# Kept weight sums of two wide gate products, requested earlier on the synchronous queue

## The chip, the cores and the metric

The kernel runs on one core of a Trainium2 chip. The metric is the device time of one execution in microseconds, as the median of several. Its engines work side by side and meet at semaphores: TensorE (PE) multiplies, ScalarE (ACT) and VectorE (DVE) prepare operands and empty the PSUM banks, GpSimd (POOL) and SyncE (SP) mostly issue DMAs.

## What is computed

One layer of an encoder on 256 positions with a model width of 2048, all in float32: a combined projection, two branches, a merge by sigmoid gates, an output projection, then a convolutional gated MLP and a final norm. The part that matters here is the gates:

```
h = rms_norm(x, g_norm)                      # 256 x 2048
proj = h @ w_in                              # 2048 x 9216
uv, qkv, gates = jnp.split(proj, [2 * GM_WIDTH, 2 * GM_WIDTH + 3 * NA_WIDTH], axis=-1)
...
g_a, g_b = jnp.split(jax.nn.sigmoid(gates), 2, axis=-1)
merged = g_a * (y_a @ w_branch[:GM_WIDTH]) + g_b * (y_b @ w_branch[GM_WIDTH:])
return x + merged @ w_out
```

Each gate has 2048 columns. The stages below compute the right halves, 1024 columns of each gate: 256 x 2048 by 2048 x 1024, twice.

## The kernel before

**Three products for one.** Every float32 operand is split into a high part (rounded by ScalarE, `whi`) and a low remainder (subtracted by VectorE, `wlo`), and a product is three matmuls: high by high, low by high, high by low (lines 317 to 319).

**A wide stage.** The right half of a gate is one call of `wide` and one of `run_wide`. Its weights come as 16 pieces, one for each 128 rows: 128 x 1024 floats, 512 KB, into one of five buffers `wraw`. Here the pieces are called a0 to a15 for the first gate and b0 to b15 for the second, in the order in which they are worked off; two neighbours with even start are a pair. Six of the eight pairs of a gate are multiplied with seven block products in place of eight, by a Strassen-Winograd scheme: it needs four sums of the pair's weight blocks (`weight_sums`, lines 360 to 364 on VectorE, split by `weight_sums_split`, lines 374 and 375) and four sums of the pair's activation blocks, the x sums. An even piece of such a pair has 9 matmuls, an odd one 12; a plain piece has 12. All eight PSUM banks are held by a stage: four for products P, four for results C. At the end of a stage `post_sums` (lines 595 to 599) and `add_sums` (line 604) empty them on ScalarE and VectorE, and the next stage starts in the banks that come free.

**What is kept.** For two pairs of each gate (pair 0 and pair 3, counted by rows of the weights) the weight sums were made and split much earlier, and written to DRAM as four tiles of 512 KB: `gate_h13`, `gate_l13`, `gate_h24`, `gate_l24`. The stage reads them back into `kh13`, `kl13`, `kh24` and `kl24`, which have one buffer each, used by all four of these pairs in turn. Of such a pair the first piece is loaded by half (256 KB). The x sums of all pairs were kept in DRAM too and are read back into three tiles s0, s1 and s2, in the turn that `GATE_TILES` gives; a tile that still holds the wanted pair is used again.

In the first gate, a2 and a3 are pair 0 and a10 and a11 are pair 3, both kept; a8 and a9 are pair 6, a12 and a13 pair 4. In the second, b2 and b3 are pair 3 and b10 and b11 are pair 0, both kept; b8 and b9 are pair 1, b12 and b13 pair 2.

**The order.** The program is written out in the order of pieces. `begin(i)` requests loads up to four pieces ahead, splits weights up to three pieces ahead, and then runs the tasks that are due at piece i. A read that is to be made n pieces ahead is a task at i - n. All these requests, weights, kept sums and x sums, go to one queue, SP's (lines 145, 1258, 1271), which issues them one after the other: a request waits until its tile is free (and until the DMA eight before it, whose semaphore it takes over, has landed), and those behind it wait too.

The leads stand in `GATE_SPLIT`: for each gate, a map from pair to three numbers, the lead of the x sums, of the tiles 13 and of the tiles 24. `wide` takes them up so:

```
ready = split[0].get(k // 2) if split else None
at(i - (ready[0] if ready else lead), ... stored(k // 2, b["acts"]))
...
    for n, lead in zip(("13", "24"), ready[-2:]):
        at(i - lead, lambda b=b, k=k, n=n: split[1](k // 2, b, n))
```

The loop uses the name `lead` again, so after a kept pair the x sums of the following pairs of the same stage are requested with that pair's last number as their lead.

Of the kernel before, what the change touches and what calls it, by code (L numbers as in the profile page):

```python
# [50 lines left out]
GATE_KEPT, GATE_MADE = (1, 2, 6), (0, 3, 4)  # L51
GATE_QUADS = ((0, 1, 2, 4, 5, 6),) * 2
GATE_ORDER = ((2, 3, 0, 1, 4, 5, 10, 11, 12, 13, 6, 7, 8, 9, 14, 15), (8, 9, 6, 7, 12, 13, 14, 15, 2, 3, 0, 1, 4, 5, 10, 11))
GATE_SPLIT = ({0: (2, 4, 3), 3: (2, 3, 2)}, {3: (2, 2, 2), 0: (4, 2, 1)})
GATE_TILES = (0, 1, 2, 0, 1, 2, 2, 1, 0)
GATE_FIRST = (40, (44, 46, 48, 48), (49, 51))
GATE_JOB = (3, (6, 6, 7, 7), (9, 12))
# [21 lines left out]
def trunk_kernel(ctx, tc, x, x_t, vecs, w_in, ln_g, ln_b, w_st, b_s, rpb, w_branch, w_out, w_up, w_down,  # L79
# [836 lines left out]
    def ev_gate_sums(br):  # L916
        def done(P, i):
            def go():
                gate_tile(br)
                mg["x", br] = [[mg["t", br][:, t, c * 512:(c + 1) * 512] for c in range(2)] for t in range(NT)]  # L920
                post_sums(P, mg["x", br], junk)

            at(i + 1, go)
        return done

    def ev_gate_wide(br):
        def done(ps, i):
            g = mg["t", br]
            add_sums(ps, mg["x", br])

            def sigmoid():
                for t in range(NT):
                    nc.scalar.activation(g[:, t, :], g[:, t, :], AF.Sigmoid, scale=st1["r"][:, t:t + 1])

            at(i + 1, sigmoid)
            for c in range(2):
                mg[br, 2 + c] = g[:, :, c * 512:(c + 1) * 512]
        return done
# [277 lines left out]
    def sums_room(name, dt):  # L1216
        return s_room["p"].tile([128, 2, 512], dt, name=name)
# [35 lines left out]
    def split_read(kept, g, tile_of, queue=nc.gpsimd):  # L1253
        def read(pair, box, n):
            u = box.setdefault("u", [])
            u.append([tile_of(pair, p + n) for p in "hl"])
            for t, src in zip(u[-1], kept[pair, g][n]):
                queue.dma_start(t.bitcast(F32), src)
            if len(u) == 2:
                split_sums(box, u)  # L1260
        return read

    def kept_sums(pair, box):
        held = [s for p, s in gate_held.values() if p == pair]
        if held:
# [10 lines left out]
                 (ev_gate_sums(br), ev_gate_wide(br)), stored=kept_sums, lead=(2, 4)[br], behind=((), (0,))[br],  # L1276
                 split=(GATE_SPLIT[br], split_read(g_kept, br, lambda pair, name: sums_room("k" + name, F32R), nc.sync)))
            for br in range(2)]
# [41 lines left out]
    def split_rows(name, pair, g):  # L1320
        return {m: [dram.tile([128, 2, 512], F32, name=f"{name}_{h}{m}_{pair}_{g}") for h in "hl"]
                for m in ("13", "24")}
# [10 lines left out]
    for n, (pair, g) in enumerate((pair, g) for g in range(2) for pair in OUT_SPLIT[g]):  # L1333
# [3 lines left out]
                    [i + a for a in OUT_JOB[2]], 4, last=True)  # L1337
    for n, (pair, br) in enumerate((pair, br) for br in range(2) for pair in GATE_SPLIT[br]):
        g_kept[pair, br] = split_rows("gate", pair, br)
# [258 lines left out]
```

## Time and profile before

| | |
|---|---|
| median of three runs | 1290.16 us (1289.01 to 1290.35) |
| the profiled execution | 1290.33 us, 1288.5 of it the span of the core |
| granted TensorE clock | 0.998 |
| TensorE busy | 1277.2 us, 99% of the span |
| VectorE, ScalarE busy | 1118.3 and 793.0 us |
| DMA moved | 369.51 MB, mean 287 GB/s |
| first wide gate stage (a0 to a15) | 373.3 to 412.7 us |
| second (b0 to b15) | 412.7 to 453.4 us |

A row of the timeline has the start in us, the duration in us, engine, line, operation, what is written and read, and in brackets the idle time before it with what ended it. For SP's queue a row is the issue of a DMA; when it landed stands in the DMA view. The row of a window has its length and then the busy time of each engine, with counts. Matmuls overlap, so their starts tell more than their durations.

### The profile page before, as it was taken

The page shows a single profiled execution, that of the slowest core. Times are in us where ns is not written, and L with a number is a line of the kernel's source. Part 1 is how long each engine was busy: PE and PEld are TensorE (multiplying, and loading weights), DVE is VectorE, ACT ScalarE, POOL GpSimd, SP SyncE. Part 2 cuts the span into 40 slices and gives each one's busy share as a digit, 9 for nine tenths or more (in the row PEclk, how much of TensorE's full clock was granted, in tenths as well). Part 3 has the DMA queues.
Part 4 walks back from the last instruction along what each step waited for, and adds up shares of the span by engine and source line. Part 5 has one row for each costly group of instructions (what it writes and reads, how often), then busy time and mean ns, then how long its engine had stood idle before and what let it go on. Part 6 is the DMA issues. An engine that isn't in the chain of part 4 may idle for free.

```text
span 1288.5 us, 19673 instructions
## 1 busy us (share of the span) xinstructions
PE 1277.2 (99%) x6717; PEld 1088.7 (84%) x6717; DVE 1118.3 (87%) x1644; ACT 793.0 (62%) x1179; POOL 162.1 (13%) x307
## 2 busy tenths in 40 slices
PE   9999999999999999999999999999999999999997
PEld 7888888888887888888888888888888888888885
DVE  7898977777799989996889999998988989979987
ACT  7776575775755655565665666665665656556654
POOL 0003852330000001100001000100000001211210
PEclk9999999999999999999999999999999999999999
DMA  9789889989789977965688789888776859998993
GB/s 364 278 272 284 288 263 345 341 284 321 247 314 360 347 238 262 387 215 179 193 281 286 239 275 304 272 260 291 261 227 219 279 174 359 374 387 321 353 392 132
DMA packets 199893, 369.51 MB, mean 287 GB/s; under 512 B 15984, under 2 KB 124144, under 8 KB 199792
## 3 DMA queue, kind: packets, MB, share of 16 engines
q1 hardware_dynamic: 175472, 286.36, 64.7%
q0 software_dynamic: 23888, 81.23, 17.7%
q8 instruction: 52, 0.85, 0.2%
q10 hardware_dynamic: 432, 0.66, 0.1%
q14 instruction: 49, 0.40, 0.1%
HBM read 320.48 MB, written 45.61 MB: 284 GB/s over the span
## 4 chain that ended last, share of the span: by engine, by line
PE 96%; DVE 2%; DMA 1%; issue 1%; DVEq 0%; ACT 0%; SPq 0%; ACTq 0%
PE bank L222 31%; PE bank L226 16%; PE bank L319 11%; PE bank L317 11%; PE bank L318 11%; PE bank L250 5%; PE bank L251 5%; PE bank L252 5%; DMA wraw<-in_w_down_dram 1%; DVE wlo L171 1%; PE bank L871 0%; PE bank L825 0%; PE bank L498 0%; PE bank L860 0%; PE bank L698 0%
## 5 line engine op out<-in xcount | busy, mean ns | idle before, releaser
L171 DVE TENSOR_TENSOR wlo<-wraw,whi 128x1024 fp32r<-128x1024 f32 (+1 forms) x472 | 537.4, 1152 | 125.0 <-ACT whi L170 74.8
L170 ACT ACTIVATE whi<-wraw 128x1024 fp32r<-128x1024 f32 (+1 forms) x472 | 463.8, 995 | 224.1 <-PE bank L318 65.1
L222 PE MATMUL bank<-h,whi 128*128 128x512 f32 x1760 | 423.3, 391 | 0.0
L222 PEld LDWEIGHTS bank<-h,whi 128*128 128x128 f32 x1760 | 322.7, 188 | 62.1
L226 PEld LDWEIGHTS bank<-h,wlo 128*128 128x128 f32 x1760 | 225.9, 191 | 8.8
L226 PE MATMUL bank<-h,wlo 128*128 128x256 f32 x1760 | 228.6, 283 | 0.0
L1076 ACT ACTIVATE tc<-ta,ck 128x256 f32<-128x256 f32 x86 | 47.1, 595 | 109.8 <-DVE ta L1074 109.8
L319 PE MATMUL bank<-wlo,a 128*128 128x512 f32 x188 | 73.4, 390 | 0.6 <-DVE wlo L171 0.6
L318 PE MATMUL bank<-whi,a 128*128 128x512 f32 x188 | 73.2, 389 | 0.0
L317 PE MATMUL bank<-whi,a 128*128 128x512 f32 x188 | 73.1, 389 | 0.0
L317 PE MATMUL bank<-whi,h 128*128 128x512 f32 x186 | 72.8, 392 | 0.0
L319 PE MATMUL bank<-wlo,h 128*128 128x512 f32 x186 | 72.6, 390 | 0.0
L318 PE MATMUL bank<-whi,h 128*128 128x512 f32 x186 | 72.6, 390 | 0.0
L1079 DVE SCALAR_TENSOR_TENSOR tc<-ta,ck,tc 128x255 f32<-128x255 f32 x86 | 41.4, 482 | 14.4 <-ACT tc L1076 14.4
L250 PE MATMUL bank<-whi,h 128*128 128x512 f32 x128 | 50.3, 393 | 0.0
L250 PE MATMUL bank<-whi,y 128*128 128x512 f32 x128 | 50.3, 393 | 0.0
L251 PE MATMUL bank<-whi,h 128*128 128x512 f32 x128 | 49.8, 389 | 0.0
L251 PE MATMUL bank<-whi,y 128*128 128x512 f32 x128 | 49.8, 389 | 0.0
L252 PE MATMUL bank<-wlo,h 128*128 128x512 f32 x128 | 49.8, 389 | 0.0
L252 PE MATMUL bank<-wlo,y 128*128 128x512 f32 x128 | 49.8, 389 | 0.0
L374 ACT ACTIVATE h<-h 128x1024 fp32r<-128x1024 f32 x36 | 38.1, 1059 | 17.5 <-DVE h L364 12.0
L1308 POOL DMA_DIRECT2D down_h<-so x16 | 8.7, 544 | 311.2 <-ACT tc L1086 184.9
(325 smaller groups left out, 1990.1 us busy)
## 6 DMA issues: line engine op xcount, KB each, us to landing
wraw<-in_w_up_dram SPq DMA_DIRECT2D x336, 256.0 KB, 4.1
wraw<-in_w_in_dram SPq DMA_DIRECT2D x107, 512.0 KB, 6.1
wraw<-in_w_down_dram SPq DMA_DIRECT2D x78, 512.0 KB, 7.5
wraw<-in_w_in_dram SPq DMA_DIRECT2D x70, 256.0 KB, 4.4
wraw<-in_w_branch_dram SPq DMA_DIRECT2D x32, 512.0 KB, 5.3
wraw<-in_w_out_dram SPq DMA_DIRECT2D x28, 512.0 KB, 5.9
h<-sums POOLq DMA_DIRECT2D x18, 512.0 KB, 7.5
tw<-in_w_down_dram POOLq DMA_DIRECT2D x8, 1024.0 KB, 8.9
```

The source lines that it names most:

```text
L170: nc.scalar.activation(h[:, k, :m], w[:, k, :m], AF.Copy)
L171: nc.vector.tensor_sub(l[:, k, :m], w[:, k, :m], h[:, k, :m].bitcast(F32))
L222: nc.tensor.matmul(p, h[:, k - k0, b * 128:(b + 1) * 128], acts(k), start=k == 0, stop=k == nk - 1)
L226: nc.tensor.matmul(p[:, :T], l[:, k - k0, b * 128:(b + 1) * 128], acts(k)[:, 0, :], start=False, stop=False)
L250: nc.tensor.matmul(p, xh, h[:, kk, :m], start=st, stop=False)
L251: nc.tensor.matmul(p, xl, h[:, kk, :m], start=False, stop=False)
L252: nc.tensor.matmul(p, xh, l[:, kk, :m], start=False, stop=sp)
L317: nc.tensor.matmul(p, xh, h, start=st, stop=False, **kw)
L318: nc.tensor.matmul(p, xl, h, start=False, stop=False, **kw)
L319: nc.tensor.matmul(p, xh, l, start=False, stop=sp, **kw)
L1076: nc.scalar.activation(v, u, AF.Identity, scale=ck[:, 1, ch:ch + 1], bias=ck[:, 3, ch:ch + 1])
L1079: nc.vector.scalar_tensor_tensor(v[:, 1:], u[:, :T - 1], ck[:, 0, ch:ch + 1], v[:, 1:], op0=OP.mult, op1=OP.add)
```

## The change

One line of numbers changes.

```
--- before
+++ after
-GATE_SPLIT = ({0: (2, 4, 3), 3: (2, 3, 2)}, {3: (2, 2, 2), 0: (4, 2, 1)})
+GATE_SPLIT = ({0: (2, 4, 3), 3: (2, 6, 5)}, {3: (2, 4, 3), 0: (4, 6, 5)})
```

The tiles 13 and 24 of the second kept pair of each gate are requested six and five pieces ahead, where it was three and two in the first gate and two and one in the second. Those of the second gate's first kept pair go four and three ahead, where it was two and two. By way of `lead`, x sums move too: those of pair 4 at a12 from two pieces ahead to five, those of pairs 6 and 1 in the second gate from two to three (pair 6 still lies in its tile and isn't read), those of pair 2 at b12 from one to five. Pair 4's x sums are now requested before pair 3's, so that these two swap the tiles s1 and s2. Instructions of TensorE, ScalarE, VectorE and POOL keep their order and number.

SP's queue in the first gate. Here `wraw` is the load of a piece (128x512 the half of a10), `kh` and `kl` the kept sums, `s` the x sums. Before, from the load of a9 to that of a13:

```order
L145 DMA wraw_4212<-in_w_in_dram 128x1024
L1271 DMA s0_4218<-xsums6_154 128x1024
L145 DMA wraw_4238<-in_w_in_dram 128x512
L145 DMA wraw_4264<-in_w_in_dram 128x1024
L1258 DMA kh13_4270<-gate_h13_3_0_140 128x1024
L1258 DMA kl13_4271<-gate_l13_3_0_141 128x1024
L145 DMA wraw_4286<-in_w_in_dram 128x1024
L1271 DMA s1_4292<-xsums3_156 128x1024
L1258 DMA kh24_4294<-gate_h24_3_0_142 128x1024
L1258 DMA kl24_4295<-gate_l24_3_0_143 128x1024
L145 DMA wraw_4307<-in_w_in_dram 128x1024
```

The same stretch now, from behind the load of a8 to that of a13:

```order
L1258 DMA kh13_4203<-gate_h13_3_0_140 128x1024
L1258 DMA kl13_4204<-gate_l13_3_0_141 128x1024
L145 DMA wraw_4216<-in_w_in_dram 128x1024
L1271 DMA s0_4222<-xsums6_154 128x1024
L1258 DMA kh24_4230<-gate_h24_3_0_142 128x1024
L1258 DMA kl24_4231<-gate_l24_3_0_143 128x1024
L145 DMA wraw_4246<-in_w_in_dram 128x512
L145 DMA wraw_4272<-in_w_in_dram 128x1024
L1271 DMA s1_4278<-xsums4_157 128x1024
L145 DMA wraw_4292<-in_w_in_dram 128x1024
L1271 DMA s2_4298<-xsums3_156 128x1024
L145 DMA wraw_4309<-in_w_in_dram 128x1024
```

The tiles 13 have moved ahead of three loads (a9, a10, a11), the tiles 24 ahead of three (a10, a11, a12), and the x sums of pair 4, which stood behind a14, ahead of a12.

SP's queue in the second gate, before, from the load of b9 to behind that of b13:

```order
L145 DMA wraw_4580<-in_w_in_dram 128x1024
L145 DMA wraw_4604<-in_w_in_dram 128x512
L1271 DMA s2_4610<-xsums1_152 128x1024
L1271 DMA s1_4620<-xsums0_155 128x1024
L145 DMA wraw_4634<-in_w_in_dram 128x1024
L145 DMA wraw_4652<-in_w_in_dram 128x1024
L1258 DMA kh13_4658<-gate_h13_0_1_148 128x1024
L1258 DMA kl13_4659<-gate_l13_0_1_149 128x1024
L145 DMA wraw_4671<-in_w_in_dram 128x1024
L1258 DMA kh24_4677<-gate_h24_0_1_150 128x1024
L1258 DMA kl24_4678<-gate_l24_0_1_151 128x1024
```

And now, from behind the load of b8 to that of b13:

```order
L1258 DMA kh13_4571<-gate_h13_0_1_148 128x1024
L1258 DMA kl13_4572<-gate_l13_0_1_149 128x1024
L145 DMA wraw_4584<-in_w_in_dram 128x1024
L1271 DMA s2_4590<-xsums1_152 128x1024
L1258 DMA kh24_4598<-gate_h24_0_1_150 128x1024
L1258 DMA kl24_4599<-gate_l24_0_1_151 128x1024
L145 DMA wraw_4614<-in_w_in_dram 128x512
L1271 DMA s1_4628<-xsums0_155 128x1024
L145 DMA wraw_4642<-in_w_in_dram 128x1024
L1271 DMA s0_4648<-xsums2_153 128x1024
L145 DMA wraw_4662<-in_w_in_dram 128x1024
L145 DMA wraw_4677<-in_w_in_dram 128x1024
```

The tiles 13 have moved ahead of four loads (b9 to b12), the tiles 24 ahead of four (b10 to b13), and the x sums of pair 2, which stood behind b15, ahead of b12. In the first pair of this gate (not shown) the tiles 13 have moved ahead of b3 and b4, the tiles 24 ahead of b4.

## The prediction

> **What bounds the kernel now.** I read the page's shares first, then the idle time in the two wide gate stages, then the queue that feeds them.
>
> The page of the kernel before:
>
> ```profile
> span 1288.5 us, 19673 instructions
> PE 1277.2 (99%) x6717; PEld 1088.7 (84%) x6717; DVE 1118.3 (87%) x1644; ACT 793.0 (62%) x1179; POOL 162.1 (13%) x307
> ```
>
> TensorE sets the time: 1288.5 - 1277.2 = 11.3 us is all that it leaves idle. The moved reads lie in the two gate stages, a0 to a15 and b0 to b15, so the question is how much of the 11.3 us is there. Busy time by stage (us, PE, PEld, DVE, ACT, POOL, clock, DMA share, GB/s), and the waits in both stages together:
>
> ```profile
> 373.30:412.70 39.40, 39.40 (x175) 32.63 (x174) 36.20 (x46) 22.33 (x25) 0.00 (x0) 1.00 0.89 325
> 412.70:453.40 40.70, 39.80 (x176) 32.56 (x175) 38.88 (x47) 23.58 (x26) 0.56 (x1) 1.00 0.93 349
> ```
>
> ```profile
> DVE t L364 <- DMA wraw<-in_w_in_dram: 2.1, 2, 1.8
> PE bank L317 <- DVE g L604: 0.9, 1, 0.9
> ```
>
> In the first gate TensorE never idles; in the second it idles once, for 0.9 us. No row has it waiting for a kept sum. Around that one stall, TensorE and VectorE by time:
>
> ```profile
> 415.20 0.39 PE L319 MATMUL bank<-l,s 128*128 128x512 f32 x1
> 416.49 0.50 PE L317 MATMUL bank<-h,s 128*128 128x512 f32 x1 [0.90 <-DVE g L604]
> ```
>
> ```profile
> 398.34 0.69 DVE L364 TENSOR_TENSOR t<-wraw 128x512 f32<-128x512 f32 x1 [1.81 <-DMA wraw<-in_w_in_dram]
> 400.27 1.22 DVE L171 TENSOR_TENSOR wlo<-wraw,whi 128x1024 fp32r<-128x1024 f32 x1
> 413.47 2.36 DVE L375 TENSOR_TENSOR l<-t,h 128x1024 fp32r<-128x1024 f32 x2
> 415.74 2.48 DVE L604 TENSOR_TENSOR g<-bank,g 128x512 f32<-128x512 f32 x4
> ```
>
> From 415.20 to 416.49 is 1.29 us, where undisturbed matmuls start 0.23 apart (380.97 and 381.20, further down), so the stall costs 1.06 us. It waits for the first of the four L604 additions, which empty the first gate's banks. That addition is late because VectorE has worked without a break since 398.34, and it started there 1.81 us late: L364 forms a sum from a12 and a13, the last pair of the first gate, and waited for the load of a13. So **one number rules this stage: when a13 lands.** Its landing comes from the synchronous queue (start, issue time; then the times to landing, in short windows, of the issues at 376.98, at 385.08 and 385.51, and at 388.23):
>
> ```profile
> 376.98 0.33 SPq L145 DMA_DIRECT2D wraw<-in_w_in_dram  x1
> 378.83 0.33 SPq L145 DMA_DIRECT2D wraw<-in_w_in_dram  x1
> 384.66 0.33 SPq L145 DMA_DIRECT2D wraw<-in_w_in_dram  x1
> 385.08 0.38 SPq L1258 DMA_DIRECT2D kh<-gate_h  x1
> 385.51 0.42 SPq L1258 DMA_DIRECT2D kl<-gate_l  x1
> 388.23 0.39 SPq L145 DMA_DIRECT2D wraw<-in_w_in_dram  x1
> ```
>
> ```profile
> wraw<-in_w_in_dram SPq DMA_DIRECT2D x1, 512.0 KB, 3.4
> ...
> kh<-gate_h SPq DMA_DIRECT2D x1, 512.0 KB, 5.9
> kl<-gate_l SPq DMA_DIRECT2D x1, 512.0 KB, 6.6
> ...
> wraw<-in_w_in_dram SPq DMA_DIRECT2D x1, 512.0 KB, 10.1
> ```
>
> The rows at 376.98, 378.83, 384.66 and 388.23 are a8, a9, a11 and a13. So kh lands at 385.1 + 5.9 = 391.0 and a13 at 388.2 + 10.1 = 398.3, six 512 KB transfers later (kl13, a12, the x sums of pair 3, kh24, kl24, a13): 7.3 / 6 = 1.22 us each, in the order of their requests.
>
> **The change part by part.** No arithmetic changes on any engine; TensorE, ScalarE and VectorE keep their instructions and their order. What moves are requests on the synchronous queue, with as many bytes in all. Four things to price.
>
> 1. *Earlier arrival of the kept sums: 0.* The first gate's second pair is used by TensorE from about 400 on. The tile views, kh and then kl:
>
> ```profile
> L318 PE MATMUL bank<-kh,s x6: 389/389/389, 380.3 to 401.4; 128*128 128x512 f32 x6
> L1258 SPq DMA_DIRECT2D kl<-gate_l x2: 402/413/424, 385.5 to 387.7; - x2
> DMA to landing us min/median/max: 6.6/8.0/9.4
> ```
>
> Three of the six matmuls stand at 380, three just before 401.4; the last of its four tiles, kl24, landed at 387.7 + 9.4 = 397.1. Nobody waited, so nothing is won directly.
>
> 2. *A new wait at the head of the queue.* kh13 is one buffer, and its previous sums (pair 0) are read by TensorE in piece a3. Now the read stands right behind a8, whose request went at 376.98, and must wait for those matmuls:
>
> ```profile
> 380.97 0.39 PE L318 MATMUL bank<-kh,s 128*128 128x512 f32 x1
> 381.20 0.39 PE L319 MATMUL bank<-kl,s 128*128 128x512 f32 x1
> ```
>
> The first frees kh13 at 380.97 + 0.39 = 381.4. Queued behind it are kl13, a9, the x sums of pair 6, kh24, kl24, a10 and the rest; a9 leaves at about 382.3 instead of 378.83. The queue meanwhile runs dry, since a8 landed at 376.98 + 3.4 = 380.4.
>
> When does a13 land now? Requests at 0.4 us steps into a queue that had run dry stand at 384.66 to 385.51; how far from full it was, against 524.3 / 1.22 = 430 GB/s when backed up, the stage row from the new read's issue on shows:
>
> ```profile
> 381.40:386.50 5.10, 5.10 (x24) 4.21 (x23) 5.10 (x6) 3.46 (x4) 0.00 (x0) 1.00 0.73 238
> ```
>
> The third of those requests landed at 385.51 + 6.6 = 392.1, 7.45 after the first issue. So the third one now, a9, lands at 381.4 + 7.45 = 388.9. Up to a13 follow s of pair 6, kh24, kl24, a10 (half), a11, s of pair 4 (moved ahead too), a12, s of pair 3 and a13: 8.5 transfers, 8.5 x 1.22 = 10.4. **a13 lands at 399.3, 1.0 us later than 398.3.** Bound below: if kh13 lands 3.4 after issue, as the lone one at 376.98 did, a13 follows it by 10.5 transfers (kl13 and a9 more): 381.4 + 3.4 + 12.8 = 397.6, 0.7 earlier. Bound above: the slowest rate of a busy stretch nearby,
>
> ```profile
> 398.00:403.00 5.00, 5.00 (x24) 4.14 (x23) 4.63 (x6) 4.54 (x5) 0.00 (x0) 1.00 1.01 401
> ```
>
> 401 GB/s, is 524.3 / 401 = 1.31 us for one: 388.9 + 11.1 = 400.0, 1.7 later. I take +1.0, the value of the row that has the same pattern of requests.
>
> What is late on the way? a9 lands at 388.9 where VectorE reached its L364 at
>
> ```profile
> 386.89 0.68 DVE L364 TENSOR_TENSOR t<-wraw 128x512 f32<-128x512 f32 x1
> 388.82 1.22 DVE L171 TENSOR_TENSOR wlo<-wraw,whi 128x1024 fp32r<-128x1024 f32 x1
> 394.10 1.83 DVE L171 TENSOR_TENSOR wlo<-wraw,whi 128x1024 fp32r<-128x1024 f32 x2 [1.19 <-ACT whi L170]
> ```
>
> ```profile
> 394.12 0.39 PE L319 MATMUL bank<-wlo,h 128*128 128x512 f32 x1
> ```
>
> so VectorE stands 2.0 us there; the 1.19 us that it idles before 394.10 and the 1.81 before 398.34 take that up again. TensorE first multiplies with a9's low part at 394.12; the subtraction at 388.82 ends at 390.0, now 392.0. From 398.34 on VectorE has no gap, so 1.0 us at a13 is 1.0 us at L604. TensorE's first need of a13 is
>
> ```profile
> 403.64 0.39 PE L319 MATMUL bank<-wlo,h 128*128 128x512 f32 x1
> ```
>
> at 403.64, against 400.27 + 1.22 = 401.5 now: 2.1 us of cover, of which 1.0 is used. The stall at 415.43 then lasts 1.06 + 1.0 instead of 1.06. Part of it shows one triple earlier, since L375's first half ends at 414.7 + 1.0, past 415.20. **+1.0 us.** If the cover of 2.1 were gone, every further tenth would stop TensorE already at a12, but it would not add to the sum: the same VectorE lateness reaches both places.
>
> 3. *The second gate's first pair* goes two pieces earlier, behind the request of b2:
>
> ```profile
> 401.52 0.33 SPq L145 DMA_DIRECT2D wraw<-in_w_in_dram  x1
> 412.73 1.06 ACT L170 ACTIVATE whi<-wraw 128x1024 fp32r<-128x1024 f32 x1 [0.24 <-ACT h L374]
> ```
>
> Its tiles 13 are free by then (the kh row above), so kh13 leaves at 401.9; b3, the third request, lands at 401.9 + 7.45 = 409.4, and b4, three on, at 413.0. ScalarE takes b3 at 412.73 and b4 behind it at 413.7, so ScalarE's own order hides both: **0**. Uncovered, b4 would cost what it comes after 413.7, and VectorE works on L375 and L604 until 418.2 before it turns to either.
>
> 4. *The second gate's second pair* repeats item 2 at b9. The tile is free at
>
> ```profile
> 421.65 0.39 PE L318 MATMUL bank<-kh,s 128*128 128x512 f32 x1
> ```
>
> that is 422.0; b9 lands at 422.0 + 7.45 = 429.5 and b13, again 8.5 transfers on, at 439.9. Before, b13 was used at
>
> ```profile
> 437.98 0.69 DVE L364 TENSOR_TENSOR t<-wraw 128x512 f32<-128x512 f32 x1 [0.33 <-DMA wraw<-in_w_in_dram]
> 439.92 1.22 DVE L171 TENSOR_TENSOR wlo<-wraw,whi 128x1024 fp32r<-128x1024 f32 x1
> ```
>
> so VectorE is 1.9 late and ends b13's low part at 443.0. TensorE's first need of it is
>
> ```profile
> 444.32 0.39 PE L319 MATMUL bank<-wlo,h 128*128 128x512 f32 x1
> ```
>
> so 1.3 us of cover is left: **0**, and beyond it one for one.
>
> **Sum:** 1290.33 (the profiled execution, 1288.5 of it the span) + 1.0 = 1291.3. The runs' median, 1290.16, lies 0.17 under the profiled one, so I predict 1291.2.
>
> **The rivals.** A measurement of this kernel can tell 0.2%, 2.6 us, from no change.
>
> *A, the queue wins.* Some of the idle time of 381.4 to 386.5 is filled now, so a13 could land early: at 397.6 (the lower bound) the stall shrinks by 0.7, and at 397.2 it is gone. For it: those 238 GB/s. Against: SP stands still for 381.4 - 378.83 = 2.6 us, and pair 4's sums now go ahead of a13. 1289.1 to 1290.3; the whole stall is 1.06, so this cannot reach 0.2%.
>
> *B, slower: the longer backlog drains slowly.* If the 8.5 transfers go at the second stage's mean rate, 349 GB/s (its row above), one takes 1.50 and a13 lands at 388.9 + 12.8 = 401.7: 3.4 late, 1293.7. It decides from a13 at 400.9, 2.6 late. Against: 1.22 measured in this very stretch. [...]
>
> *C, the second gate gives way.* b13 more than 1.3 us later than worked out (past 441.2), and TensorE stops in b12 for the rest: +0.5 to +2, on top of item 2, 1291.8 to 1293.3.
>
> *D, the reads are not the matter at all:* the queue absorbs the block and a13 lands within 0.2 of before: 1290.2.
>
> **How the numbers follow.** Forecast 0.50, A 0.15, B 0.12, C 0.08, D 0.12; 0.03 for a gain that no row here shows. The forecast, A, D and half of C are within 0.2%: 0.50 + 0.15 + 0.12 + 0.04 = 0.81. B and the other half of C are slower: 0.16. Faster: 0.03. The range runs from A's 1289.2 to 1293.2, inside which most of C lies and B begins. The likeliest case alone, from the bounds -0.7 and +1.7 of item 2, is 1289.5 to 1291.9.
>
> **What would show it.** Right: in the changed profile the kh read leaves near 381.4 and a9 about 382.3; L364 of a13 begins near 399.3 with the wait before it on the load; TensorE stops near 415 for about 2 us and nowhere else in the two stages. Wrong: a stall of TensorE in a8 to a12 or b8 to b13 (a load later than I count), a stall near 415 under 0.5 us (A), or a kh read that leaves before 381 (the tile was free earlier than I think).

## The result

The changed kernel takes 1292.56 us (median of 15 runs, 1290.96 to 1294.59), the kernel before 1290.16 (15 runs beside them, 1289.01 to 1291.36). The ratio is 1.0017, with a 95% interval of 1.0009 to 1.0025: a loss of 0.1 to 0.25%, within what I had called no change, and more than twice the 1.0 us that I had forecast.

The profiled execution took 1292.56 us, 1290.8 of it the span. The waits of TensorE in the whole of it:

```profile
PE bank L498 <- DVE one L488: 1.5, 1, 1.5
PE bank L317 <- DVE g L604: 1.2, 1, 1.2
PE bank L319 <- DVE l L375: 0.5, 1, 0.5
PE bank L319 <- DVE wlo L171: 0.2, 1, 0.2
```

The one wait for L604 has grown from 0.9 to 1.2 us, and in front of it stands one for L375, 0.5 us, that was not there. The last row lies near the end of the program, at 1273.7 us, where before has one of 0.6 us; it has nothing to do with the gates. TensorE by time, first three rows of before, then the changed kernel:

```profile
414.97 0.39 PE L318 MATMUL bank<-h,s 128*128 128x512 f32 x1
...
418.92 0.40 PE L318 MATMUL bank<-whi,h 128*128 128x512 f32 x1
419.15 0.39 PE L319 MATMUL bank<-wlo,h 128*128 128x512 f32 x1
```

```profile
414.57 0.39 PE L318 MATMUL bank<-h,s 128*128 128x512 f32 x1
415.48 0.50 PE L319 MATMUL bank<-l,s 128*128 128x512 f32 x1 [0.52 <-DVE l L375]
417.21 0.50 PE L317 MATMUL bank<-h,s 128*128 128x512 f32 x1 [1.23 <-DVE g L604]
...
419.33 0.63 PE L317 MATMUL bank<-h,h 128*128 128x512 f32 x1
419.76 0.63 PE L318 MATMUL bank<-h,h 128*128 128x512 f32 x1
420.19 0.63 PE L319 MATMUL bank<-l,h 128*128 128x512 f32 x1
...
421.04 0.56 PE L318 MATMUL bank<-whi,h 128*128 128x512 f32 x1
421.44 0.39 PE L319 MATMUL bank<-wlo,h 128*128 128x512 f32 x1
```

Up to 414.6 the changed execution is 0.40 us ahead (from the start: the second L317 stands at 6.14 us, against 6.52 before). At 417.21, against 416.49 before, it is 0.72 behind: the stall is 1.1 us longer. At 421.44, against 419.15, it is 2.29 behind, though nothing waits in between: **the matmuls from 418 to 421.4 start 0.43 us apart, where they start 0.23 apart elsewhere.** The stage rows say why (after the times of the engines: granted clock, DMA share, GB/s):

```profile
414.00:418.00 4.00, 2.24 (x9) 1.26 (x8) 4.00 (x6) 0.34 (x2) 0.00 (x0) 1.00 0.68 225
418.00:421.40 3.40, 3.40 (x9) 2.70 (x9) 3.40 (x6) 3.04 (x3) 0.28 (x1) 0.50 0.16 20
421.40:425.00 3.60, 3.60 (x17) 2.93 (x16) 3.57 (x5) 2.73 (x3) 0.28 (x1) 1.00 0.79 266
```

The clock is halved for 3.4 us behind the stall. So 2.29 + 0.40 = 2.7 us arise here: 1.1 of stall and 1.6 of half clock. The runs show both cases. Six of the 15 executions kept a mean clock of 0.998 or more, and took 1290.96 to 1291.51 us; nine had 0.996 or 0.997, and took 1292.23 to 1294.59. The medians of the two groups, 1291.0 and 1293.3 us, lie 2.3 us apart, more than the 1.6 us of the profiled execution; where the rest comes from isn't in a trace.

Where the stall comes from, in VectorE's rows of the changed kernel and in SP's:

```profile
387.38 0.69 DVE L364 TENSOR_TENSOR t<-wraw 128x512 f32<-128x512 f32 x1 [0.81 <-DMA wraw<-in_w_in_dram]
399.07 0.69 DVE L364 TENSOR_TENSOR t<-wraw 128x512 f32<-128x512 f32 x1 [0.42 <-DMA wraw<-in_w_in_dram]
414.20 2.35 DVE L375 TENSOR_TENSOR l<-t,h 128x1024 fp32r<-128x1024 f32 x2
416.47 2.48 DVE L604 TENSOR_TENSOR g<-bank,g 128x512 f32<-128x512 f32 x4
```

```profile
380.99 0.33 SPq L1258 DMA_DIRECT2D kh<-gate_h  x1
381.41 0.38 SPq L1258 DMA_DIRECT2D kl<-gate_l  x1
381.89 0.37 SPq L145 DMA_DIRECT2D wraw<-in_w_in_dram  x1
```

With the 0.40 us added that this execution is ahead, kh13 leaves at 381.4 and a9 at 382.3, to the tenth as worked out, and L364 of a13 begins at 399.5 against 398.34.

### The profile page after: what moved, and what is told of

Read it like the earlier page. It is cut to its first block, busy times and chain, and to the rows that moved or that the text cites. A ratio compares the mean times of both kernels' runs of the same rounds, so it can differ in the third digit from the quotient of the medians.

```text
span 1290.8 us, 19673 instructions
## 1 busy us (share of the span) xinstructions
PE 1278.9 (99%) x6717; PEld 1089.6 (84%) x6717; DVE 1118.5 (87%) x1644; ACT 793.7 (61%) x1179; POOL 162.9 (13%) x307
## 4 chain that ended last, share of the span: by engine, by line
PE 90%; DVE 4%; DMA 4%; issue 1%; DVEq 0%; ACT 0%; SPq 0%; ACTq 0%
PE bank L222 31%; PE bank L226 16%; PE bank L319 9%; PE bank L317 9%; PE bank L318 9%; PE bank L250 5%; PE bank L251 5%; PE bank L252 5%; DMA wraw<-in_w_down_dram 2%; DVE wlo L171 2%; DMA wraw<-in_w_in_dram 1%; DVE h L375 0%; DVE h L364 0%; PE bank L871 0%; PE bank L825 0%
## 5 line engine op out<-in xcount | busy, mean ns | idle before, releaser
L317 PE MATMUL bank<-whi,a 128*128 128x512 f32 x188 | 73.2, 389 | 0.0
L317 PE MATMUL bank<-whi,h 128*128 128x512 f32 x186 | 72.8, 392 | 0.0
L374 ACT ACTIVATE h<-h 128x1024 fp32r<-128x1024 f32 x36 | 38.0, 1059 | 16.5 <-DVE h L364 10.3
```

The costliest lines, as they stand in the source:

```text
L317: nc.tensor.matmul(p, xh, h, start=st, stop=False, **kw)
```

## The experiments

My theory after the two traces: a13 lands 1.1 us later, VectorE hands that on to the emptying of the banks, TensorE stalls 2.2 us instead of 1.06, and a stall of that length lets the clock fall in part of the executions. The rivals: the second gate's reads cost the time; or, within the first gate, it is the kept reads' wait at the head of SP's queue, or else the x sums of pair 4, which the change moved only because a loop uses the name `lead` twice. Every run is compared with the kernel before on the same chip: 1290.1 us (33 runs) for the first four, 1290.46 (27 runs) for the last three.

### One gate at a time

```
-GATE_SPLIT = ({0: (2, 4, 3), 3: (2, 3, 2)}, {3: (2, 2, 2), 0: (4, 2, 1)})
+GATE_SPLIT = ({0: (2, 4, 3), 3: (2, 6, 5)}, {3: (2, 2, 2), 0: (4, 2, 1)})
```

> Only the first gate's numbers are changed (its second kept pair six and five pieces ahead, and with it pair 4's x sums five ahead); the second gate's are those of before. Theory (a13 lands about 1.1 us later, VectorE passes that on to the emptying of the banks, TensorE stalls 2.2 us instead of 1.06 near 415, and the clock is halved for some 3.4 us in part of the executions): the whole loss is here, 1291.2 to 1292.6 us, with a stretch at half clock behind the stall in the profile or without it. Rival (the second gate's reads do it): 1290.2 us and the stall of before.

Measured: 1291.14 us (11 runs, 1290.83 to 1293.44), ratio 1.0012 [1.0003, 1.0021]. Its profile has the stall of the changed kernel, and the half clock behind it:

```profile
415.65 0.50 PE L319 MATMUL bank<-l,s 128*128 128x512 f32 x1 [0.50 <-DVE l L375]
417.39 0.62 PE L317 MATMUL bank<-h,s 128*128 128x512 f32 x1 [1.23 <-DVE g L604]
```

Three of the 11 executions had a clock of 0.997 or less (1292.6 to 1293.4 us); the other eight took 1290.83 to 1291.83. Both groups lie where those of the whole change lie. The median, just under the range expected, is lower because fewer executions lost their clock.

```
-GATE_SPLIT = ({0: (2, 4, 3), 3: (2, 3, 2)}, {3: (2, 2, 2), 0: (4, 2, 1)})
+GATE_SPLIT = ({0: (2, 4, 3), 3: (2, 3, 2)}, {3: (2, 4, 3), 0: (4, 6, 5)})
```

> Only the second gate's numbers are changed. Theory: nothing but the short stall at b13 of the changed kernel, 0.2 to 0.3 us, so 1290.2 to 1290.5 us, full clock at 415 to 425. Rival (the second gate's reads do it): 1291.3 to 1292.6 us with a stall of 1 us or more in b8 to b13.

Measured: 1289.98 us (11 runs, 1289.31 to 1291.56), ratio 1.0001 [0.9992, 1.0009]. The profile has short waits of 0.2 us at b9 and b13,

```profile
440.00 0.50 PE L319 MATMUL bank<-wlo,h 128*128 128x512 f32 x1 [0.17 <-DVE wlo L171]
445.26 0.50 PE L319 MATMUL bank<-wlo,h 128*128 128x512 f32 x1 [0.20 <-DVE wlo L171]
```

which cost less than the runs can tell. So the added stall, and a loss of clock behind it, come with the first gate's numbers alone. That three of 11 executions lost their clock there and nine of 15 in the whole change may be chance: so few runs don't show whether the second gate's numbers play a part in that.

### The kept reads or the x sums

The whole change, with the loop's name mended so that each x sum is requested where it was before:

```
-                for n, lead in zip(("13", "24"), ready[-2:]):
-                    at(i - lead, lambda b=b, k=k, n=n: split[1](k // 2, b, n))
+                for n, ahead in zip(("13", "24"), ready[-2:]): at(i - ahead, lambda b=b, k=k, n=n: split[1](k // 2, b, n))
+                lead = X_LEAD.get((c0, k // 2), ahead)
```

where `X_LEAD` holds the old numbers, 2 for the pair 3 of either gate and 1 for the second gate's pair 0.

> All kept sums are read as early as in the change, but every x sum is requested where it was before (pair 4's behind a14 again). Theory: one 512 KB transfer less ahead of a13, so a13 lands 1.2 us earlier than in the changed kernel, within 0.2 of before; stall 0.9 to 1.2 us, no half clock; 1290.0 to 1290.6 us. Rival (the wait of the kept reads at the head of the queue is what costs): a13 stays late, 1291.3 us or more.

Measured: 1290.0 us (11 runs, 1289.5 to 1290.39), ratio 0.9999 [0.999, 1.0008]; the clock kept in every one. VectorE starts on a13 at 398.15, and the stall is 0.5 us, less than the 0.9 to 1.2 expected:

```profile
398.15 0.69 DVE L364 TENSOR_TENSOR t<-wraw 128x512 f32<-128x512 f32 x1
```

```profile
416.29 0.50 PE L317 MATMUL bank<-h,s 128*128 128x512 f32 x1 [0.50 <-DVE g L604]
```

All the kept reads are requested as early as in the change (from 384 to 386 us data moved at 404 GB/s, against 391 in the change and 118 before), and nothing is lost.

The opposite: the kernel before, in which only `X_LEAD = {(GA0 + 1024, 3): 5}` moves pair 4's x sums.

> The kernel before with one thing changed: pair 4's x sums are requested five pieces ahead of a12 instead of two, so ahead of a12's load. Theory: a13 lands 1.2 us later than before, the stall near 415 grows to about 2.2 us, the clock halves behind it in part of the executions: 1291.2 to 1292.6 us, the same as the whole change. Rival (the kept reads do it): 1290.2 us.

Measured: 1291.74 us (11 runs, 1290.71 to 1293.81), ratio 1.0014 [1.0005, 1.0023]. Its VectorE and TensorE:

```profile
399.56 0.69 DVE L364 TENSOR_TENSOR t<-wraw 128x512 f32<-128x512 f32 x1 [2.77 <-DMA wraw<-in_w_in_dram]
```

```profile
415.97 0.50 PE L319 MATMUL bank<-l,s 128*128 128x512 f32 x1 [0.34 <-DVE l L375]
417.70 0.50 PE L317 MATMUL bank<-h,s 128*128 128x512 f32 x1 [1.23 <-DVE g L604]
```

a13 is waited for 0.96 us longer than before (2.77 against 1.81), and the stall is that of the changed kernel. In this execution the clock held, though the stall is nearly the same as in the first experiment; four of the 11 had 0.997 or less. One 512 KB transfer put ahead of the load of a13 is enough for the loss of the first gate.

### Freeing the load that rules

If a13's landing rules the stage, it should pay to put something behind it. The kernel before, with the tiles 24 of pair 3 requested one piece later (the x sums held in place by `X_LEAD`):

```
-GATE_SPLIT = ({0: (2, 4, 3), 3: (2, 3, 2)}, {3: (2, 2, 2), 0: (4, 2, 1)})
+GATE_SPLIT = ({0: (2, 4, 3), 3: (2, 3, 1)}, {3: (2, 2, 2), 0: (4, 2, 1)})
```

> The kernel before with the tiles 24 of the first gate's second kept pair requested one piece ahead in place of two, which puts these two transfers behind a13; all x sums as before. Theory (a13's landing rules the stage): a13 lands 2.4 us earlier, near 395.9, VectorE does not wait for it, the banks are empty 1 us or more earlier and the stall of 1.06 us near 415 is gone: 1289.0 us, faster than before by 0.9 to 1.3 us. The tiles 24 then land near 398.3, TensorE reads them from 401.1 on. Rival (the stall has another cause, or the later tiles bring one of their own): 1290.1 us or more.

Measured: 1288.88 us (11 runs, 1288.26 to 1289.95), ratio 0.999 [0.9981, 0.9999]. It is the fastest of the kernels here, 1.6 us under the kernel before, where 0.9 to 1.3 was expected; the stall explains 1.06 of it. In the profile TensorE waits for nothing in either gate stage, and VectorE takes a13 without a gap:

```profile
396.09 0.69 DVE L363 TENSOR_TENSOR t<-wraw 128x512 f32<-128x512 f32 x1
396.69 0.69 DVE L364 TENSOR_TENSOR t<-wraw 128x512 f32<-128x512 f32 x1
...
414.39 2.48 DVE L604 TENSOR_TENSOR g<-bank,g 128x512 f32<-128x512 f32 x4
```

The change had read the kept sums earlier, and what gain there is, 0.1%, lay in reading half of the first gate's later.

### What halves the clock

No DMA changes here; VectorE gets idle work on scratch, ahead of the first gate's bank emptying: `nc.vector.tensor_add(junk, junk, junk)`, once and three times.

> The kernel before with one more VectorE addition (128x512 on scratch, 0.6 us) just ahead of the first gate's bank emptying; no DMA changes. Theory: the stall near 415 becomes 1.06 + 0.6 = 1.66 us; 1290.7 us with the clock kept, and if a stall of this length already halves the clock, 1.5 us more in some of the executions, up to 1292.3. Rival (the half clock of the changed kernel comes from something in the DMAs): 1290.7 in all executions.

Measured: 1290.44 us (11 runs, 1289.74 to 1291.24), ratio 1.0 [0.9991, 1.0009]; the clock held in all 11. In the profile

```profile
416.50 0.50 PE L317 MATMUL bank<-h,s 128*128 128x512 f32 x1 [1.12 <-DVE g L604]
```

the idle time is 1.1 us instead of 0.9: in this execution a13 was waited for 1.44 us and not 1.81, which took back most of the addition. So the stall of 1.66 us that I expected was not there to be seen, and the interval of 1.2 us either way would not have shown 0.6.

> The same with three additions: a stall of 1.06 + 1.8 = 2.9 us. Theory: the clock is halved for some 3.4 us behind the stall in most executions, so 1290.1 + 1.8 + 1.5 = 1293.4 us. Rival (the half clock comes from the DMAs): 1291.9 us, full clock.

Measured: 1293.92 us (11 runs, 1291.66 to 1294.8), ratio 1.0024 [1.0015, 1.0033]; ten of the 11 had a clock of 0.997 or less, and the one that kept 0.998 took 1291.66.

```profile
418.26 0.80 PE L317 MATMUL bank<-h,s 128*128 128x512 f32 x1 [3.04 <-DVE g L604]
```

```profile
418.20:421.50 3.30, 3.24 (x8) 2.58 (x9) 3.30 (x6) 2.62 (x3) 0.00 (x0) 0.50 0.16 60
```

A stall that VectorE alone makes has the same half clock behind it, so this belongs to the stall and not to the DMAs. By the idle time in the profiled execution of each kernel: 0.9 to 1.1 us, none of 71 executions lost their clock (before and one addition, of those listed with their clock); 0.3 to 0.5 and then 1.2 us within 2.2, sixteen of 37 (the changed kernel, the first gate alone, the x sums alone); 3.0 us, ten of 11.

Why does a stall of one length take the clock down in some executions only? In the changed kernel the half clock lasts from 417.98 to 421.39 us. These are the 3.41 us before it and the half clock itself, then the same in the first gate alone:

```profile
414.57:417.98 3.41, 1.65 (x6) 0.78 (x5) 3.41 (x5) 0.19 (x1) 0.00 (x0) 1.00 0.63 195
417.98:421.39 3.41, 3.41 (x9) 2.72 (x9) 3.41 (x6) 3.06 (x3) 0.27 (x1) 0.50 0.16 20
414.21:417.62 3.41, 1.68 (x7) 0.86 (x6) 3.41 (x5) 0.00 (x0) 0.00 (x0) 1.00 1.03 410
417.62:421.04 3.42, 3.42 (x9) 2.63 (x9) 3.42 (x6) 3.03 (x3) 0.00 (x0) 0.50 0.69 278
```

And these are two stretches of that length that hold the stall of the x sums alone, where the clock stayed full:

```profile
413.43:416.84 3.41, 2.70 (x11) 1.69 (x9) 3.38 (x5) 1.15 (x2) 0.00 (x0) 1.00 1.01 402
416.84:420.26 3.42, 2.56 (x11) 2.08 (x12) 3.42 (x6) 1.94 (x2) 0.00 (x0) 1.00 1.00 407
```

Before the fall TensorE idles for 1.76 and 1.73 us of the 3.41 (3.41 - 1.65 and 3.41 - 1.68). In the x sums alone it idles for 0.71 and 0.86 us, 1.57 in all, and the clock holds. The other profiles lie on either side: with three additions it idles for 2.99 us from 414 to 418.2 (busy for 1.21 of 4.20) and the clock falls; with waits for L604 of 0.5 to 1.1 us (the x sums as before, before, the second gate alone, one addition) it holds. That is one execution of each kernel. Whether the 0.16 to 0.19 us between 1.57 and the other two decided it, or the time at which the stall came, isn't shown, and neither is why executions of one kernel differ.

## Why the prediction was right, and where it was not

**The bound and the ruling number held.** That the landing of a13 sets the stall of the stage is shown from both sides: later by one transfer (x sums alone) the stall grows, earlier by two (tiles 24 later) it is gone.

**Item 1, nothing direct from earlier kept sums:** held, and shown by the run with the x sums in place, 1290.0 against 1290.1.

**Item 2, the stall: the size held, the clock was missed.** a13 was worked out 1.0 us late and came 1.1 late; the stall grew by 1.1 us, part of it one triple earlier, at L375, as written. The step that failed is the sum "+1.0 us", which took the stall's own length for its whole cost. The recovery behind it was left at the 0.50 and 0.40 us rows of before, and I did not ask what a longer stall does to the clock. It cost 1.6 us in the profiled execution, and nine of 15 runs lost their clock, which is why the median moved 2.4 and not 1.0. The executions that kept their clock, 1290.96 to 1291.51, are at the forecast 1291.2.

Two terms inside item 2 were off and cancelled, so that a13's time was met partly by luck. a9 lands at

```profile
wraw<-in_w_in_dram SPq DMA_DIRECT2D x1, 512.0 KB, 5.5
```

381.89 + 5.5 = 387.4, with the 0.4 us of lead 387.8, and not at 388.9: three requests into an empty queue took 6.4 us here and not 7.45. What the earlier row had in excess appears two transfers on, where kh24 lands 2.4 us after the x sums that it follows in place of 1.22:

```profile
s<-xsums SPq DMA_DIRECT2D x1, 512.0 KB, 6.3
kh<-gate_h SPq DMA_DIRECT2D x1, 512.0 KB, 8.2
```

(382.32 + 6.3 = 388.6 and 382.83 + 8.2 = 391.0.) And the cause within item 2 was named too broadly. I put the wait at the queue's head first and pair 4's sums in the count. The run with the x sums in place shows that the early reads alone do no harm: L364 of a13 begins at 398.15 there, against 398.34 before.

**Item 3** held: no wait of TensorE from 421 to 444. **Item 4** counted 1.3 us of cover at b13, and there was none:

```profile
446.42 0.39 PE L318 MATMUL bank<-whi,h 128*128 128x512 f32 x1
446.76 0.50 PE L319 MATMUL bank<-wlo,h 128*128 128x512 f32 x1
447.10 0.40 PE L317 MATMUL bank<-whi,s 128*128 128x512 f32 x1
```

TensorE takes b13's low part 0.1 us late and loses 0.2 us by it, too little for a row among the waits and for the runs to resolve. By the prediction's own list of signs, a stall in b8 to b13 spoke against the forecast; this one is small, but the margin was 1.4 us less than worked out. With the 2.29 us taken off by which this execution is behind, b13's load lands at 433.60 + 9.2 - 2.29 = 440.5 and not at 439.9, and VectorE comes to it late, since it waited twice for ScalarE's splits of weights just before (2.0 and 0.9 us). Why it waits so long there wasn't tried.

**The rivals.** A did not occur in the change, but the run with the x sums in place is close to it: a stall of 0.5 us. B's time, 1293.7, is in the neighbourhood of the executions that lost their clock, for another reason: the queue did not drain slowly, 10.3 us from a13's request to its landing against 10.1 before. C gave 0.2 us instead of 0.5 to 2. D was wrong, the stall moved by 1.1 us.

## What to carry to other kernels

In a queue that is backed up, a request for something nobody waits for is paid by the load behind it: here one 512 KB transfer ahead of a13 made VectorE wait 0.96 us longer for it, and two put behind it took the stall of 1.06 us away. Find the one load that rules the stage, and move the reads with slack behind it, not ahead. Where a stall of TensorE grows beyond the 1.1 us that left the clock alone here, count the time at half clock behind it as well (1.6 us in the profiled execution), and look for it in the granted clock of each execution. And before pricing a change of a few numbers, follow every use of them: here a loop variable carried one of them on to requests of another kind, and the whole loss was theirs.

## What the runs showed of the hardware that I had not expected

A stall of TensorE in two parts, 0.5 and 1.2 us, had 3.4 us of half clock behind it in the profiled execution of the change, which cost 1.6 us, more than the added stall itself (1.1 us). In the profiles here the clock fell where TensorE had idled for 1.73 and 1.76 of the last 3.41 us (the first gate alone, the change), and held where its stall came to 1.57 us (the x sums alone).

In a backed-up queue, where transfers land 1.22 us apart, one step stands out that ends at 391.0 us: 2.3 us before, from a11 (384.66 + 4.0 = 388.7) to kh13 (385.08 + 5.9 = 391.0), and 2.4 us in the change, from the x sums of pair 6 (388.6) to kh24 (391.0). It falls on a kept tile both times, though not on the same one. The queue doesn't pause there: data moved at 411 GB/s from 387.5 to 391 us before and at 408 in the change. Its cause wasn't tried.
